# RWKV's low-rank products as two 128-row passes with stored high and low halves, and a gated-delta matrix without its mask

## The chip, the core and the metric

One core of a Trainium2 chip runs the whole program. The metric is device time in microseconds, the median of several executions. TensorE (PE in the profile) does the matrix products, VectorE (DVE) and ScalarE (ACT) the elementwise work, GpSimd (POOL) some small elementwise work, and SyncE (SP) only issues DMA transfers, one after the other in the order of its program. An instruction that waits on an engine holds up everything that stands behind it on that engine; on SP this holds for the transfers behind a waiting transfer.

## What is computed

One layer over 512 positions of width 2048: an input projection, two kinds of sequence mixer side by side (gated delta, 8 heads of 128; RWKV-7, 16 heads of 64, handled here in 8 pairs), an output projection, cross-attention and an MLP. The two places that the change touches:

```python
# RWKV: two low-rank products, rank 64 each
w_log = -softplus(-(w0 + tanh(w_lo) @ w2)) - 0.5
a = sigmoid(a0 + a_lo @ a2)

# gated delta, per chunk: a unit lower triangular system, M strictly lower
gamma = where(causal, exp(where(causal, diff, 0.0)), 0.0)
M = where(strict, einsum("bhnid,bhnjd->bhnij", kb, kc) * gamma, 0.0)
sol = triangular_solve(M + eye, rhs, lower=True, unit_diagonal=True)
```

All data is f32. Big products use an f32r type of matmul and are made of three: each operand is split into a part that f32r holds (high) and the rest (low), and high·high, high·low and low·high are summed.

## The kernel before

The first part of the program, some 1000 us, is one long input projection with the mixers woven into it. The projection is 59 columns of 128 outputs (`py`), each of 16 x 3 matmuls of 128x512 on PE; a column's raw weights come in two halves of 512 KB (`wraw`, three buffers), and ACT and DVE split each half into `whi` and `wlo` (two buffers each) before PE can use it. Seven columns belong to each of eight rounds: three for a pair of RWKV heads, `rwkv(j)`, and four for a gated-delta head, `gdn(h)`. Rounds 1 to 5 are alike.

The order of the instructions in this part isn't written by hand. `run()` is a greedy planner: each stage is a generator of operations, and the planner always takes the one that could start first by its own cost estimates (`cost()`, `start()`, `issue()`), so any change of one operation can move others on all engines, SP's transfers included. On the chip each engine then simply runs its list in that order and waits where an input isn't there yet.

The parts that the prediction follows, in one round:

- `rwkv(j)` loads a 128x128 piece of the stacked weights w2 and a2 (`lw`) and makes `pW` and `pA` by one f32 matmul each over 64 rows: `wa` holds tanh(w_lo) in its upper and a_lo in its lower 64 rows. Later it forms `pgA` and `pgB` on PE, masks them on DVE into `GA` and `GB`, and stores blocks of them to DRAM (`ndri`).
- `inverse_blocks` solves the 16x16 diagonal blocks on POOL. For RWKV: blocks are loaded from DRAM (`sr<-ndri`), POOL works through 15 steps, the results go out to DRAM (`bg16T`, `bg16U`) and come back rearranged (`r<-bg16T` twice, `E<-bg16U` four times). For gated delta the same road has the names `ndgi`, `sgi`, `bg8T`, `bg8U`, `gk<-bg8T`, `gqn<-bg8U`.
- `gdn(h)` turns decays into `E` (exponentials, zero where the row index is above the column index), multiplies it on POOL by the constant `sneg` (minus one strictly above the diagonal, else zero) into `Es`, forms `pkk` on PE and writes the product `NTm = pkk * Es` on DVE (tile name `gEs`). `NTm` goes to DRAM as `ndgi` and through POOL's solve.
- `inverse_levels` joins the solved blocks on PE. Its first products, `gj0x` to `gj7x` by head, need `gk`, the tile that came back from `bg8T`. Since PE runs its list in order, everything behind `gjNx`, the projection too, waits if `gk` isn't there.
- `rs`, `gs`, `po`, `gpo` are the serial recurrences of the mixers, interleaved one by one with projection matmuls.

After this part come the keys and queries of cross-attention (`kp`, `kq`), then the rest, whose order is not touched.

Lines that carry what was just told:

```python
yield TE.matmul(pW, lw[0:64, :], wa[0:64, :], start=True, stop=True)
yield TE.matmul(pA, lw[64:128, :], wa[64:128, :], start=True, stop=True)
```

Of the kernel before, what the change touches and what calls it, by code (L numbers as in the profile page):

```python
# [9 lines left out]
F32 = mybir.dt.float32  # L10
F32R = mybir.dt.float32r
# [6 lines left out]
P = 128  # L18
# [7 lines left out]
CST = {}  # L26
_off = 0
for _n, _w in (("ident", 128), ("ones", 128), ("mA", 128),
               ("lv64", 2 * 64), ("cen", 64), ("sneg", 128), ("mbias", 128),
               ("rst64", 512)):  # L30
    CST[_n] = (_off, _w)
    _off += _w
# [13 lines left out]
def constants():  # L46
    c = np.zeros((P, NCST), np.float32)

    def put(name, a):
        o, w = CST[name]  # L50
        c[:, o:o + w] = a

    i = np.arange(P)
    put("ident", np.eye(P))
    put("ones", 1.0)
    j = np.arange(64)
    st = (j[:, None] < j[None, :]).astype(np.float32)
    inc = (j[:, None] <= j[None, :]).astype(np.float32)
    put("mA", np.tile(np.concatenate([st, inc], 1), (2, 1)))

    def level(n, s):
        a = np.arange(n)
        blk = a[:, None] // (2 * s) == a[None, :] // (2 * s)
        return (blk & (a[:, None] % (2 * s) >= s) & (a[None, :] % (2 * s) < s)).astype(np.float32)

    put("lv64", np.concatenate([np.tile(level(64, 16 << l), (2, 1)) for l in range(2)], 1))
    put("cen", np.tile(np.eye(64) - 1.0 / 64, (2, 1)))
    put("sneg", -(i[:, None] < i[None, :]).astype(np.float32))
    put("mbias", np.where(i[:, None] <= i[None, :], 1e30, -1e30))
    put("rst64", np.tile((np.arange(512) % 64 != 0).astype(np.float32), (P, 1)))  # L70
    return c


def build(tc, I, out):
# [178 lines left out]
    def after(*ev):  # L253
        return lambda: ev in events
# [362 lines left out]
    def rows():  # L617
        R = tl("gE")
        yield DV.memset(R, 0.0)
        rs128 = tl("bon")  # L620
        g8 = slice(32, 40)
        ab, b16 = slice(32, 48), slice(64, 80)
        yield after("rstd")
        yield AC.activation(nA, col("alog"), AF.Exp)
        yield DV.tensor_scalar(out=nA, in0=nA, scalar1=-1.0, scalar2=None, op0=ALU.mult)
        yield DV.memset(rs128[g8, :], 1.0)
        for c in range(4):
            yield DV.memset(rs128[g8, c * P:c * P + 1], 0.0)
# [24 lines left out]
        yield AC.activation(e_[g8, :], e_[g8, :], AF.Ln, bias=b_one[g8, :])
        yield DV.scalar_tensor_tensor(out=x_[g8, :], in0=x_[g8, :], scalar=0.0, in1=e_[g8, :],
                                      op0=ALU.max, op1=ALU.add)
        yield DV.tensor_scalar(out=x_[g8, :], in0=x_[g8, :], scalar1=nA[g8, :], scalar2=None, op0=ALU.mult)
        yield DV.tensor_tensor_scan(out=R[g8, :], data0=rs128[g8, :], data1=x_[g8, :], initial=0.0,
                                    op0=ALU.mult, op1=ALU.add)
        R3 = R.rearrange("p (c t) -> p c t", t=P)
        tail = tl("gqn")  # L660
        t3 = tail.rearrange("p (c t) -> p c t", t=P)
        yield DV.tensor_tensor(out=t3[g8], in0=R3[g8, :, P - 1:P].broadcast_to([8, 4, P]),
                               in1=R3[g8], op=ALU.subtract)
        yield AC.activation(R[96:104, :], tail[g8, :], AF.Exp)
        yield DV.tensor_scalar(out=R[b16, :], in0=R[b16, :], scalar1=0.5, scalar2=0.5, op0=ALU.mult, op1=ALU.add)
        pt = psb("prt", "scg", 1)
        for c in range(4):
            yield TE.transpose(pt[:, c * P:(c + 1) * P], R[:, c * P:(c + 1) * P], ident)
        yield SY.dma_start(Rd, R[32:96, :])
        yield DV.tensor_copy(RT, pt.rearrange("p (c a b) -> p c a b", a=4, b=32)[:, :, 1:4, 0:16])  # L670
# [41 lines left out]
        blk = z.rearrange("(q u) -> q u", u=1040)[:, 0:1024].rearrange("q (r c) -> q r c", c=64)[:, :, 0:16]  # L712
        return full, blk

    def inverse_blocks(nm, store, m, tags, temps, ready, out, moved=False):


        np_ = 4 * m
# [11 lines left out]
        for j in range(15):  # L730
            w = 15 - j
            t = s2[0:np_, 0:w * (j + 1)].rearrange("p (a b) -> p a b", b=j + 1)
            yield GS.tensor_tensor(out=t, in0=D[:, j, j + 1:16].unsqueeze(2).broadcast_to([np_, w, j + 1]),
                                   in1=Td[:, j:j + 1, 0:j + 1].broadcast_to([np_, w, j + 1]), op=ALU.mult)
            yield GS.tensor_tensor(out=Td[:, j + 1:16, 0:j + 1], in0=Td[:, j + 1:16, 0:j + 1], in1=t, op=ALU.add)
        Ud = D
        yield GS.tensor_copy(Ud, Td.rearrange("p a b -> p b a"))
        solving.pop()
# [16 lines left out]
    def inverse_levels(nm, Tm, Tt, NT, tags, mx, big):  # L755
# [4 lines left out]
        for l in range(2):  # L760
# [13 lines left out]
                  for r, c in HI if r == 0 or l == 0]  # L774
            yield from pairs(tl_ + up, th)
            rr = slice(0, P) if l == 0 else hA
            yield DV.tensor_tensor(out=Tm[rr, 0:2], in0=Tm[rr, 0:2], in1=d[rr, 4:6], op=ALU.add)
            yield DV.tensor_tensor(out=Tm[rr, 2:4], in0=Tm[rr, 2:4], in1=o[rr, 0:2], op=ALU.add)
            if l == 0:
                yield DV.tensor_tensor(out=Tt, in0=Tt, in1=d[:, 0:4], op=ALU.add)  # L780
                continue
            for r in (1, 0):
                w = slice(r * 64, r * 64 + 64)
                for c, h in ((slice(0, 2), HALF[r]), (slice(2, 4), HALF[1 - r])):
                    yield DV.tensor_tensor(out=big[HALF[r], c, w], in0=Tt[h, c], in1=d[h, c], op=ALU.add)


    def rwkv(j):
        base = 3 + 7 * j
        js = slice(j * P, (j + 1) * P)  # L790
        lw = tl("lw", P)
        yield SM.dma_start(lw, I["w2a2"][:, js])
        c3 = lambda a: a.rearrange("p (c t) -> p c t", t=64)
        yield after("lowrank")
        yield after("zeros")
        pW, pA = psb(f"pW{j}"), psb(f"pA{j}")
        yield TE.matmul(pW, lw[0:64, :], wa[0:64, :], start=True, stop=True)
        yield TE.matmul(pA, lw[64:128, :], wa[64:128, :], start=True, stop=True)
        tw = short()
        yield AC.activation(tw, pW, AF.Tanh, scale=0.5, bias=hw0[:, j:j + 1])  # L800
        tA = tl("tA")
# [155 lines left out]
        if j < 7:  # L957
            chain(rwkv(j + 1), 3)

        lgs = tile_of(pm, [P, 3 * P], F32R, "lgs", f"lgs{j}", 1)  # L960
        yield AC.copy(lgs[0:96, 0:2 * P], lg[0:96, :])
        yield AC.copy(lgs[96:128, 0:P], lg[96:128, 0:P])
        yield DV.tensor_tensor(out=lgs[:, 2 * P:3 * P], in0=lg[:, 0:P], in1=lgs[:, 0:P].bitcast(F32), op=ALU.subtract)
# [46 lines left out]
    def gdn(h):  # L1010
# [42 lines left out]
            yield DV.scalar_tensor_tensor(out=E[:, cs], in0=E[:, cs], scalar=RT[:, c, 0, h:h + 1],  # L1053
                                          in1=K("mbias"), op0=ALU.subtract, op1=ALU.min)
        yield AC.activation(E, E, AF.Exp)
        Es = tl("gEs")
        yield GS.tensor_tensor(out=c3(Es), in0=c3(E), in1=K("sneg").unsqueeze(1).broadcast_to([P, 4, P]), op=ALU.mult)
        kn = yield from normed(k_, None, "gkn", 0)
        kb = tl("gk")
        yield DV.tensor_tensor(out=kb, in0=kn, in1=B, op=ALU.mult)  # L1060
# [1 line left out]
        for c in range(4):  # L1062
            cs = slice(c * P, (c + 1) * P)
            yield TE.matmul(pkk[:, cs], kn[:, cs], kb[:, cs], start=True, stop=True)
        NTm = Es
        yield DV.tensor_tensor(out=NTm, in0=pkk, in1=Es, op=ALU.mult)

        def store(full):
            yield SY.dma_start(full[:, 0:4, :], c3(NTm)[hA, :, 0:64])
# [1 line left out]

        inv = []
        chain(inverse_blocks(f"gi{h}", store, 8, ("gkn", "gk", "gqn"), lambda: (tl("sgi"), tl("sgj", 240)),
                             after("gq", h), inv, True), 1, ("gi", h))
        if h:
            yield after("gs", h - 1)
        q_ = yield from conv(1, 0, "gq")
# [43 lines left out]
        for c in range(4):  # L1121
            yield TE.matmul(p4[hB, c * 64:(c + 1) * 64], N3[hA, c, 64:128], Tm[hA, c, :], start=True, stop=True)
        Y = tl("gkn")
        yield DV.tensor_copy(Y[hB, 0:256], p4[hB, 0:256])
        p5 = psb(f"gi{h}z", "mg")
        for c in range(4):
            yield TE.matmul(p5[hA, c * 64:(c + 1) * 64], Y[hB, c * 64:(c + 1) * 64], TtG[hB, c, 64:128],
# [918 lines left out]
```

## Time and profile before

| | us |
|---|---|
| median of 3 runs | 2886.73 |
| lowest, highest | 2885.18, 2887.63 |
| the profiled execution | 2890.1 |
| its span in the trace | 2888.3 |
| PE busy in it | 2865.6 |
| DVE, ACT, POOL busy | 2224.1, 1557.9, 312.5 |

The profile comes from one execution, which took 2890.1 us, 3.4 us more than the median; 1.8 us of it lie outside the span. In timelines the columns are start, duration, engine, line, operation, out<-in and count; `SPq` rows are SP issuing transfers. A fp32 matmul shows as two passes, an f32r matmul as one. Starts of neighbouring PE rows show throughput; the durations overlap. Line 228 (`issue`) is the planner's, so almost all of the first part has that line, and rows are told apart by tile names.

### The profile page before, as it was taken

The page shows a single profiled execution, that of the slowest core. Times are in us where ns is not written, and L with a number is a line of the kernel's source. Part 1 is how long each engine was busy: PE and PEld are TensorE (multiplying, and loading weights), DVE is VectorE, ACT ScalarE, POOL GpSimd, SP SyncE. Part 2 cuts the span into 40 slices and gives each one's busy share as a digit, 9 for nine tenths or more (in the row PEclk, how much of TensorE's full clock was granted, in tenths as well). Part 3 has the DMA queues.
Part 4 walks back from the last instruction along what each step waited for, and adds up shares of the span by engine and source line. Part 5 has one row for each costly group of instructions (what it writes and reads, how often), then busy time and mean ns, then how long its engine had stood idle before and what let it go on. Part 6 is the DMA issues. An engine that isn't in the chain of part 4 may idle for free.

```text
span 2888.3 us, 48119 instructions
## 1 busy us (share of the span) xinstructions
PE 2865.6 (99%) x18458; PEld 2412.0 (84%) x18458; DVE 2224.1 (77%) x3379; ACT 1557.9 (54%) x2254; POOL 312.5 (11%) x704
## 2 busy tenths in 40 slices
PE   8999999999999999999999999999999999999998
PEld 7888887888877888889888888888888888888887
DVE  7676676676767767769866898888998896878786
ACT  7454644644646555664455555555555654454444
POOL 0302203213123000001111100010010000000000
PEclk9999999999999999999999999999999999999999
DMA  5423323323424479787788767888777888776765
GB/s 193 112 83 95 99 79 103 93 72 104 114 86 143 155 245 299 261 307 201 206 219 215 187 193 220 229 235 248 215 205 209 290 274 267 222 262 210 252 190 178
DMA packets 304503, 546.64 MB, mean 189 GB/s; under 512 B 97224, under 2 KB 178380, under 8 KB 303248
## 3 DMA queue, kind: packets, MB, share of 16 engines
q1 hardware_dynamic: 245264, 449.17, 49.0%
q0 software_dynamic: 35840, 67.12, 11.7%
q10 hardware_dynamic: 23168, 27.27, 2.6%
q8 instruction: 145, 2.38, 0.3%
q14 instruction: 86, 0.70, 0.1%
HBM read 479.10 MB, written 131.48 MB: 211 GB/s over the span
## 4 chain that ended last, share of the span: by engine, by line
PE 97%; DMA 1%; DVE 1%; POOL 0%; ACT 0%; issue 0%; SPq 0%; ACTq 0%; POOLq 0%
PE py L228 22%; PE upx L1334 8%; PE upx L1336 4%; PE upy L1334 4%; PE dx L1801 4%; PE dx L1800 4%; PE dx L1803 4%; PE vp L122 3%; PE sc L122 3%; PE at L122 3%; PE vo L122 3%; PE kp L228 3%; PE kq L228 3%; PE upy L1336 2%; PE dy L1803 2%; PE dy L1801 2%
## 5 line engine op out<-in xcount | busy, mean ns | idle before, releaser
L130 ACT CAST whi<-ub 128x1024 fp32r<-128x1024 f32 x290 | 304.8, 1052 | 283.8 <-PE dy L1801 62.7
L131 DVE TENSOR_TENSOR wlo<-ub,whi 128x1024 fp32r<-128x1024 f32 x290 | 352.8, 1220 | 63.2 <-ACT whi L130 57.7
L228 PE MATMUL py<-xhi,whi 128*128 128x512 f32 x928 | 374.0, 403 | 7.7 <-ACT xhi L228 7.7
L228 PE MATMUL py<-xlo,whi 128*128 128x512 f32 x928 | 371.2, 400 | 0.0
L228 PE MATMUL py<-xhi,wlo 128*128 128x512 f32 x912 | 363.0, 398 | 0.0
L130 ACT CAST whi<-ua 128x1024 fp32r<-128x1024 f32 x205 | 215.6, 1052 | 195.9 <-PE dx L1801 70.8
L228 ACT CAST whi<-wraw 128x1024 fp32r<-128x1024 f32 (+1 forms) x180 | 187.1, 1039 | 234.6 <-PE py L228 149.4
L131 DVE TENSOR_TENSOR wlo<-ua,whi 128x1024 fp32r<-128x1024 f32 x205 | 249.9, 1221 | 53.4 <-ACT whi L130 52.7
L228 DVE TENSOR_TENSOR wlo<-wraw,whi 128x1024 fp32r<-128x1024 f32 (+1 forms) x178 | 217.6, 1222 | 89.0 <-ACT whi L228 87.6
L1334 PE MATMUL upx<-cb,whi 128*128 128x512 f32 x992 | 250.1, 394 | 0.0
L228 PEld LDWEIGHTS py<-xhi,whi 128*128 128x128 f32 x928 | 174.9, 189 | 48.1 <-ACT xhi L228 7.7
L1334 PEld LDWEIGHTS upx<-cb,whi 128*128 128x128 f32 x992 | 178.5, 189 | 32.5 <-DVE sl L1292 0.4
L228 PEld LDWEIGHTS py<-xlo,whi 128*128 128x128 f32 x928 | 175.1, 189 | 34.5 <-DVE xlo L228 0.7
L228 PEld LDWEIGHTS py<-xhi,wlo 128*128 128x128 f32 x912 | 171.9, 188 | 35.8 <-issue 1.0
L1800 PE MATMUL dx<-whi,dh 128*128 128x512 f32 x480 | 186.8, 389 | 0.0
L1801 PE MATMUL dx<-whi,dl 128*128 128x512 f32 x480 | 186.7, 389 | 0.0
L1336 PEld LDWEIGHTS upx<-cb,wlo 128*128 128x128 f32 x992 | 135.3, 190 | 9.8
L1336 PE MATMUL upx<-cb,wlo 128*128 128x256 f32 x992 | 138.3, 282 | 0.0
L131 DVE TENSOR_TENSOR wlo<-wr,whi 128x1024 fp32r<-128x1024 f32 x80 | 97.8, 1224 | 43.7 <-ACT whi L130 42.7
L1803 PE MATMUL dx<-wlo,dh 128*128 128x512 f32 x480 | 128.6, 389 | 0.0
L228 ACT ACT_TABLE_LOAD x84 | 107.8, 1283 | 35.4 <-DVE suml_gon L228 14.5
L1334 PE MATMUL upy<-cb,whi 128*128 128x512 f32 x496 | 124.3, 392 | 0.0
(903 smaller groups left out, 6681.7 us busy)
## 6 DMA issues: line engine op xcount, KB each, us to landing
ws<-in_w_dn POOLq DMA_DIRECT2D x128, 512.0 KB, 7.4
wraw<-in_w_in SPq DMA_DIRECT2D x116, 512.0 KB, 3.8
ua<-in_w_dn SPq DMA_DIRECT2D x108, 512.0 KB, 4.4
ub<-in_w_up SPq DMA_DIRECT2D x71, 512.0 KB, 6.2
ua<-in_w_up SPq DMA_DIRECT2D x56, 512.0 KB, 4.8
ub<-in_w_dn SPq DMA_DIRECT2D x52, 512.0 KB, 4.6
sl<-cd SPq DMA_DIRECT2D x104, 256.0 KB, 5.0
ub<-ws SPq DMA_DIRECT2D x52, 512.0 KB, 4.3
```

What stands on the lines that cost most here:

```text
L122: PE.matmul(o, l, r, start=start, stop=stop)
L130: tie(S.copy(hi, src))
L131: V.tensor_tensor(out=lo, in0=src, in1=hi.bitcast(F32), op=ALU.subtract)
L228: f(*a, **k)
L1334: PE.matmul(pt, hi[:, k * P:k * P + P], parts[k], start=start and k == 0, stop=False, skip_group_check=True)
L1336: PE.matmul(pt[:, HA], lo[:, k * P:k * P + P], parts[k][:, HA], start=False, stop=k == 7, skip_group_check=True)
L1800: PE.matmul(pts[t], uh[:, x], hi[:, w], start=start and z == 0 and q == 0, stop=False, skip_group_check=True)
L1801: PE.matmul(pts[t], ul[:, x], hi[:, w], start=False, stop=False, skip_group_check=True)
L1803: PE.matmul(pts[t], uh[:, x], lo[:, w], start=False, stop=z == 1 and q == 3, skip_group_check=True)
```

## The change

Two things. First, the low-rank products: `wa` becomes a temporary, and two new f32r tiles hold high and low activations stacked in 128 rows, `LXA` (high part of a_lo in one half of the rows, low part in the other) and `LXW` likewise for tanh(w_lo). The weights are loaded twice, once into each half of the rows, so `lw` is 128x256 and takes four transfers of 64x128 instead of one, and is split into high and low (`lws`: one cast on ACT, one subtraction on DVE). `pW` and `pA` are two f32r matmuls over 128 rows each: weights' high part times the stacked activations, then their low part times the same.

Second, the mask of the gated-delta matrix: `sneg`, its constant columns and POOL's product `Es` go; `NTm = pkk * E` keeps the diagonal and has the other sign. Neither is read wrongly: the solves use only entries strictly above the diagonal of a block, and the signs move into subtractions in place of additions and a multiplication by -1 in place of a copy.

```diff
-    wa = pq.tile([P, T], F32, name="wa")
+    LXW, LXA = (pq.tile([P, T], F32R, name=n) for n in ("LXW", "LXA"))
...
+        wa = tl("gqd")
         yield from shiftmix(0, 0, wa)
         yield AC.activation(wa[0:64, :], wa[0:64, :], AF.Tanh)
+        for x, a, b in ((LXA, hB, hA), (LXW, hA, hB)):
+            yield AC.copy(x[a], wa[a])
+            yield DV.tensor_tensor(out=x[b], in0=wa[a], in1=x[a].bitcast(F32), op=ALU.subtract)
...
-            yield GS.tensor_tensor(out=Td[:, j + 1:16, 0:j + 1], in0=Td[:, j + 1:16, 0:j + 1], in1=t, op=ALU.add)
+            yield GS.tensor_tensor(out=Td[:, j + 1:16, 0:j + 1], in0=Td[:, j + 1:16, 0:j + 1], in1=t, op=op)
...
-        lw = tl("lw", P)
-        yield SM.dma_start(lw, I["w2a2"][:, js])
+        lw = tl("lw", 2 * P)
+        for z, a in enumerate(HALF):
+            for b in HALF:
+                yield SM.dma_start(lw[b, z * P:z * P + P], I["w2a2"][a, js])
+        lws = tile_of(pm, [P, 4 * P], F32R, "lws", f"lws{j}", 1)
+        yield from split_(lw, lws[:, 0:2 * P], lws[:, 2 * P:4 * P])
...
-        yield TE.matmul(pW, lw[0:64, :], wa[0:64, :], start=True, stop=True)
-        yield TE.matmul(pA, lw[64:128, :], wa[64:128, :], start=True, stop=True)
+        for z, (p_, x) in enumerate(((pW, LXW), (pA, LXA))):
+            for n in (0, 1):
+                w = (2 * n + z) * P
+                yield TE.matmul(p_, lws[:, w:w + P], x, start=n == 0, stop=n == 1)
...
-        Es = tl("gEs")
-        yield GS.tensor_tensor(out=c3(Es), in0=c3(E), in1=K("sneg").unsqueeze(1).broadcast_to([P, 4, P]), op=ALU.mult)
...
-        NTm = Es
-        yield DV.tensor_tensor(out=NTm, in0=pkk, in1=Es, op=ALU.mult)
+        NTm = tl("gEs")
+        yield DV.tensor_tensor(out=NTm, in0=pkk, in1=E, op=ALU.mult)
...
-        yield DV.tensor_copy(Y[hB, 0:256], p4[hB, 0:256])
+        yield DV.tensor_scalar(out=Y[hB, 0:256], in0=p4[hB, 0:256], scalar1=-1.0, scalar2=None, op0=ALU.mult)
```

The planner makes a new order of all this. Three places show it. Names have a running number behind them, which differs between the two programs.

On PE, the low-rank products of RWKV's fifth pair, among the first steps of the recurrence of the fourth. Before:

```order
L228 MATMUL py_5323<-xhi_376,wlo_5244 128x512
L228 MATMUL pW_5548<-wa,lw_5546 128x512
L228 MATMUL rs_3_0_5556<-BK_4861,BTz 128x64
L228 MATMUL pA_5549<-wa,lw_5546 128x512
L228 MATMUL py_5323<-xhi_387,whi_5325 128x512
```

Now:

```order
L227 MATMUL gi3y<-gk_5285,gEs_5088 64x64 x3
L227 MATMUL rs_3_1_5628<-Qs_5049,WTz 128x64
L227 MATMUL gi3y<-gk_5285,gEs_5088 64x64
L227 MATMUL pW_5633<-LXW,lws_5606 128x512 x2
L227 MATMUL pA_5634<-LXA,lws_5606 128x512
L227 MATMUL rs_3_1_5638<-BK_4966,BTz 128x64
L227 MATMUL gi3z<-TtG,gkn_5631 64x64 x4
L227 MATMUL pA_5634<-LXA,lws_5606 128x512
```

Two f32 products became four f32r ones, and a step `rs` now stands inside the group `gi3y`, which was whole before.

On SP, the transfers around the end of RWKV's solve and the start of gated delta's in the fourth round. Before:

```order
L228 DMA wraw_4946<-in_w_in 128x1024
L228 DMA bg16T<-sr_4712 64x16x16
L228 DMA bg16U<-sr_4712 64x16x16
L228 DMA r_4953<-bg16T 64x8x64 x2
L228 DMA E_288_4954<-bg16U 64x4x64 x4
L228 DMA wraw_5001<-in_w_in 128x1024
L228 DMA ndgi_5036<-gEs_4892 64x4x64 x2
L228 DMA wraw_5055<-in_w_in 128x1024
L228 DMA sgi_5045<-ndgi_5036 32x16x16
```

Now:

```order
L227 DMA bg16T<-sr_4816 64x16x16
L227 DMA bg16U<-sr_4816 64x16x16
L227 DMA wraw_5047<-in_w_in 128x1024
L227 DMA lg_5063<-in_g2a 128x128
L227 DMA lg_5063<-in_g2b 32x128 x3
L227 DMA r_5051<-bg16T 64x8x64 x2
L227 DMA E_288_5052<-bg16U 64x4x64 x4
L227 DMA wraw_5107<-in_w_in 128x1024
L227 DMA ndgi_5118<-gEs_5088 64x4x64 x2
L227 DMA sgi_5125<-ndgi_5118 32x16x16
```

The five transfers `wraw` and `lg`, which stood ahead of `bg16T`, now stand between `bg16U` and `r`; the `wraw` between `ndgi` and `sgi` is gone. The same rows stand in rounds 2 to 5; in rounds 0 and 1 `lg` stays ahead of `bg16T`.

On DVE, the product that writes `NTm` (tile `gEs`) in the same round. Before:

```order
L228 TENSOR_TENSOR gkn_5003<-gk_4637,sg_4963 128x512
L228 TENSOR_TENSOR gk_5017<-gkn_5003,gqe_4380 128x512
L228 TENSOR_TENSOR gEs_4892<-pkk_5022,gEs_4892 128x512
```

Now:

```order
L227 TENSOR_TENSOR gkn_5055<-gk_4650,sg_4883 128x512
L227 TENSOR_TENSOR gk_5072<-gkn_5055,gqe_4424 128x512
L227 TENSOR_TENSOR y_212<-py_4885,rstd 128x512
L227 TENSOR_TENSOR wlo_5094<-wraw_4828,whi_5093 128x1024
L227 TENSOR_TENSOR gEs_5088<-pkk_5079,gE_4423 128x512
```

An eviction of a projection column and a weight split now stand ahead of it.

Counted on PE in that round: between the last matmul of the second `pgA`/`pgB` group and `pkk` stood 101 f32r matmuls of 128x512, and now 79; between `pkk` and the first `gj3x` stood 123, and now 118. The other groups of matmuls between these points are the same ones. Summed over both stretches, before and now: round 0 227 and 179, round 1 224 and 188, rounds 2 to 5 224 and 197, round 6 220 and 217. In round 1 the groups `ris`, `rit` and `riu` of RWKV now stand ahead of `gj1x` too. The whole program has 12 ACT rows more, of them two table loads.

More of the change, by code (lines that the diff above doesn't have):

```diff
@@ L28 @@
 for _n, _w in (("ident", 128), ("ones", 128), ("mA", 128),
-               ("lv64", 2 * 64), ("cen", 64), ("sneg", 128), ("mbias", 128),
+               ("lv64", 2 * 64), ("cen", 64), ("mbias", 128),
                ("rst64", 512)):
@@ L67, in constants @@
     put("cen", np.tile(np.eye(64) - 1.0 / 64, (2, 1)))
-    put("sneg", -(i[:, None] < i[None, :]).astype(np.float32))
     put("mbias", np.where(i[:, None] <= i[None, :], 1e30, -1e30))
@@ L713, in views, with inverse_blocks @@
         return full, blk
-    def inverse_blocks(nm, store, m, tags, temps, ready, out, moved=False):
+    def inverse_blocks(nm, store, m, tags, temps, ready, out, moved=False, op=ALU.add):
         np_ = 4 * m
@@ L776, in inverse_levels @@
             rr = slice(0, P) if l == 0 else hA
-            yield DV.tensor_tensor(out=Tm[rr, 0:2], in0=Tm[rr, 0:2], in1=d[rr, 4:6], op=ALU.add)
-            yield DV.tensor_tensor(out=Tm[rr, 2:4], in0=Tm[rr, 2:4], in1=o[rr, 0:2], op=ALU.add)
+            yield DV.tensor_tensor(out=Tm[rr, 0:2], in0=Tm[rr, 0:2], in1=d[rr, 4:6], op=ALU.subtract)
+            yield DV.tensor_tensor(out=Tm[rr, 2:4], in0=Tm[rr, 2:4], in1=o[rr, 0:2], op=ALU.subtract)
             if l == 0:
-                yield DV.tensor_tensor(out=Tt, in0=Tt, in1=d[:, 0:4], op=ALU.add)
+                yield DV.tensor_tensor(out=Tt, in0=Tt, in1=d[:, 0:4], op=ALU.subtract)
                 continue
@@ L784, in inverse_levels @@
                 for c, h in ((slice(0, 2), HALF[r]), (slice(2, 4), HALF[1 - r])):
-                    yield DV.tensor_tensor(out=big[HALF[r], c, w], in0=Tt[h, c], in1=d[h, c], op=ALU.add)
+                    yield DV.tensor_tensor(out=big[HALF[r], c, w], in0=Tt[h, c], in1=d[h, c], op=ALU.subtract)
     def rwkv(j):
@@ L958, in rwkv @@
             chain(rwkv(j + 1), 3)
-        lgs = tile_of(pm, [P, 3 * P], F32R, "lgs", f"lgs{j}", 1)
+        lgs = tile_of(pm, [P, 3 * P], F32R, "lgs", f"lg_s{j}", 1)
         yield AC.copy(lgs[0:96, 0:2 * P], lg[0:96, :])
@@ L1073, in gdn @@
         chain(inverse_blocks(f"gi{h}", store, 8, ("gkn", "gk", "gqn"), lambda: (tl("sgi"), tl("sgj", 240)),
-                             after("gq", h), inv, True), 1, ("gi", h))
+                             after("gq", h), inv, True, ALU.subtract), 1, ("gi", h))
         if h:
```

## Prediction

> **What bounds the kernel now.** I read the page first: how busy each engine is, and the chain of work that ended last.
>
> ```profile
> PE 2865.6 (99%) x18458; PEld 2412.0 (84%) x18458; DVE 2224.1 (77%) x3379; ACT 1557.9 (54%) x2254; POOL 312.5 (11%) x704
> PE 97%; DMA 1%; DVE 1%; POOL 0%; ACT 0%; issue 0%; SPq 0%; ACTq 0%; POOLq 0%
> ```
>
> PE is the bound: work taken off PE is time won, work on another engine is free until PE waits for it. So the second view is PE's own waits.
>
> ```profile
> PE py L228 <- ACT xhi L228: 7.7, 1, 7.7
> PE gj6x L228 <- DMA gk<-bg8T: 3.1, 1, 3.1
> ```
>
> Besides the start there is one wait worth a name: in round 6 PE stood 3.1 us before `gj6x`, until gated delta's solved blocks came back from DRAM. The mixers' latency thus already touches PE once. The third view gives busy times by stretch, here a steady round from `pkk` to the next `pkk` (columns: stretch, its length, busy us and count of PE, PEld, DVE, ACT, POOL, then the granted clock).
>
> ```profile
> 453.45:564.53 111.08, 111.08 (x1031) 90.31 (x1030) 75.62 (x141) 57.74 (x79) 24.30 (x67) 1.00 0.32 92
> ```
>
> A round takes 111.1 us, and PE is never idle in it. The question is twofold: how much PE work goes, and whether the new order leaves the chain that ends in `gk` enough time.
>
> **PE work.** PE around the low-rank products of one round:
>
> ```profile
> 497.66 0.39 PE L228 MATMUL py<-xhi,wlo 128*128 128x512 f32 x1
> 497.98 1.12 PE L228 MATMUL pW<-wa,lw 64*128 64x512 f32 x2
> 499.03 0.43 PE L228 MATMUL rs<-BK,BTz 128*128 128x64 f32 x2
> ...
> 500.45 0.50 PE L228 MATMUL py<-xhi,whi 128*128 128x512 f32 x1
> 500.79 0.40 PE L228 MATMUL py<-xlo,whi 128*128 128x512 f32 x1
> 501.02 0.40 PE L228 MATMUL py<-xhi,wlo 128*128 128x512 f32 x1
> 501.26 0.33 PE L228 MATMUL rs<-Qs,WTz 128*128 128x64 f32 x2
> 501.52 0.67 PE L228 MATMUL gi3y<-gk,gEs 64*64 64x64 f32 x8
> ```
>
> An f32r product of 128x512 takes 0.233 us from start to start (500.79 to 501.02). From 497.66 to 500.79 are 3.13 us; without two `py` (0.47) and one `rs` (0.26 by the row at 501.26) the two old products, `pW` and the `pA` that follows `rs`, cost 2.4 us. Four new ones, of the very form of `py`, take 0.93. That saves 1.47. A change to or from a row group of 64 costs about 0.1 (497.66 to 497.98 is 0.32, not 0.23); the `rs` that now splits `gi3y` adds two, and with its lost overlap I take 0.27 back. **1.2 us a round, 9.6 in eight.**
>
> **The chain that ends in `gk`.** One round on SP, DVE and PE, before:
>
> ```profile
> 426.05 0.69 DVE L228 TENSOR_TENSOR GA<-pgA,cst 128x512 f32<-128x512 f32 x1 [0.53 <-PE pgA L228]
> 436.48 0.42 SPq L228 DMA_DIRECT2D lg<-in_g2a  x1
> 436.94 1.43 SPq L228 DMA_DIRECT2D lg<-in_g2b  x3
> 447.00 0.59 SPq L228 DMA_DIRECT2D bg16T<-sr  x1
> 447.68 0.62 SPq L228 DMA_DIRECT2D bg16U<-sr  x1
> 449.76 1.27 SPq L228 DMA_DIRECT2D r<-bg16T  x2
> 451.14 2.55 SPq L228 DMA_DIRECT2D E<-bg16U  x4
> 453.74 0.60 SPq L228 DMA_DIRECT2D wraw<-in_w_in  x1
> 453.46 0.72 PE L228 MATMUL pkk<-gk,gkn 128*128 128x128 f32 x5
> 454.62 0.69 DVE L228 TENSOR_TENSOR gEs<-pkk,gEs 128x512 f32<-128x512 f32 x1 [1.50 <-PE pkk L228]
> 455.34 1.26 SPq L228 DMA_DIRECT2D ndgi<-gEs  x2
> 459.31 0.34 SPq L228 DMA_DIRECT2D sgi<-ndgi  x1
> 476.09 0.34 SPq L228 DMA_DIRECT2D bg8T<-sgi  x1
> 479.14 1.26 SPq L228 DMA_DIRECT2D gk<-bg8T  x2
> 484.77 0.23 PE L228 MATMUL gj3x<-gk,gEs 64*64 64x64 f32 x2
> gk<-bg8T SPq DMA_DIRECT2D x16, 64.0 KB, 2.4
> ```
>
> The reader is to see three things. RWKV's solve leaves POOL 20.95 us after `GA` starts (426.05 to 447.00), and SP then is bound to that solve's four kinds of transfer until 453.74, behind which `ndgi` stands; `NTm` is done only at 455.3, so this costs nothing. From `ndgi` to the landing of the second `gk` transfer (479.14 + 0.64 + 2.4 = 482.2) pass 26.9 us. PE reaches `gj3x` at 484.77: 2.6 us to spare.
>
> Now the order. Between `pgA` and `pkk` stand 22 f32r products fewer, 5.1 us: `pkk` comes 22.3 us after `GA` (before 27.4), that is, `bg16T` 1.3 us ahead of `pkk` instead of 6.5. Behind it SP has, by its rows' steps, `bg16U` 0.7, `wraw` 0.4, `lg` 1.9, `r` 1.4, `E` 2.6, `wraw` 0.4 (the 0.38 of the row at 790.04 below): with 0.7 from `bg16T` to `bg16U`, `ndgi` issues 6.7 us after `pkk`, where it was 1.9. That `NTm` itself stands behind an eviction and a split on DVE changes nothing, since SP comes later still. Then 26.9 us as before: `gk` lands 33.6 us after `pkk`. PE arrives at `gj3x` 31.3 us after `pkk` less five products (1.2), at 30.1. **PE waits 3.4 us a round in rounds 2 to 5**, and `py` waits behind it. Whatever else PE should wait for between `pgA` and `gj3x` is part of this sum, not added to it.
>
> Rounds 0 and 1 lose more products over both stretches, 45 and 36 below the 224 of a steady round where rounds 2 to 5 lose 27, but `lg` (1.9 us) is out of the way there; I take the same 3.4. In all six rounds **20 us**.
>
> Bounds of this wait: had the chain its old slack in full, zero, and then nothing is paid; 1 us more a round if `ndgi` lands late behind the `wraw` issued just ahead of it. Round 6 shows that such a delay exists:
>
> ```profile
> 787.92 0.60 SPq L228 DMA_DIRECT2D wraw<-in_w_in  x1
> 788.62 1.32 SPq L228 DMA_DIRECT2D wraw<-in_memT  x1
> 790.04 0.38 SPq L228 DMA_DIRECT2D wraw<-in_w_in  x1
> 790.50 1.33 SPq L228 DMA_DIRECT2D ndgi<-gEs  x2
> 798.17 0.34 SPq L228 DMA_DIRECT2D sgi<-ndgi  x1
> 820.60:824.10 3.50, 3.50 (x78) 2.63 (x82) 1.06 (x3) 0.69 (x1) 0.00 (x0) 0.57 0.23 46
> ```
>
> Three loads of 512 KB just ahead of `ndgi`, and its landing released `sgi` 7.7 us later instead of 4.0. So came the 3.1 us wait, and behind it 3.5 us at a granted clock of 0.57 (the column behind the busy times), worth 3.5 x 0.43, some 1.5 us. In the new order round 6 keeps 217 of 220 products and gains groups of RWKV ahead of `gj6x`, so I take this event, **4.6 us**, as gone and leave 1 us for what remains of it.
>
> The clock term: waits of 3.4 us are as long as the one that dropped the clock. From none to all six of them could drop it, 0 to 9 us; I take half, **4.5**.
>
> [...]
>
> **The rest.** The `lw` loads and the split:
>
> ```profile
> L228 SPq DMA_DIRECT2D lw<-in_w2a x8: 328/432/432, 11.0 to 826.4; - x8
> L228 ACT CAST lgs<-lg x16: 293/349/408, 163.6 to 933.5; 96x256 fp32r<-96x256 f32 x8, 32x128 fp32r<-32x128 f32 x8
> L228 DVE TENSOR_TENSOR lgs<-lg,lgs x16: 282/292/383, 164.6 to 934.8; 128x128 fp32r<-128x128 f32 x8, 32x128 fp32r<-32x128 f32 x8
> 447.62 1.28 POOL L228 TENSOR_TENSOR gEs<-gE,cst 128x512 f32<-128x512 f32 x1
> L228 ACT ACT_TABLE_LOAD x84 | 107.8, 1283 | 35.4 <-DVE suml_gon L228 14.5
> ```
>
> Three more `lw` issues take 1.3 us of SP a round, a cast near 0.35 us of ACT and a subtraction of 0.3 to 0.7 of DVE (its twice as wide form lies between the quoted row and the 0.69 of `GA`). ACT with 54% and DVE with 77% busy hide them, at zero. The cast waits for `lw`, and weight casts wait behind it, so `py` would pay if `lw` came late; 0 to 1 us a round, I take zero, since `pW` now stands later in its round. The two casts and two subtractions of `LXA` and `LXW` at the start, near 2.6 us at most in series, delay the first `pW` by ten products in PE's order, filled with `py`: zero, or 2.6 without that cover. Two table loads, 2.6 us of ACT: zero. The mask's 1.28 us on POOL stood between the two solves, and the second begins only when `sgi` has landed, 14 us later: no gain. Copy for multiplication, addition for subtraction: the same cost.
>
> **Sum**, against the profiled 2890.1 (span 2888.3, 1.8 outside): -9.6 + 20 - 4.6 + 1 + 4.5 = +11.3, so 2901.4 in a profile. The median of the runs is 3.4 lower: **2898.0**.
>
> **The rivals.**
> - *The waits come, but the clock holds*: +6.8, 2893.5. Against it, the clock row of round 6. [...]
> [...]
> - *The chain is covered, and only PE work counts* (not slower, but faster): the mechanism is SP between `bg16T` and `ndgi`. If `ndgi` issues under 3.3 us after `pkk`, 3.4 earlier than worked out, because the first solve leaves POOL earlier, the waits vanish: -9.6 - 4.6 + 1 = -13.2, 2873.5. For it: PE's old slack of 2.6 us. Against it: five transfers more stand there by the order, and POOL runs the same 15 steps.
> - That the new products don't run as four of 0.233 is excluded by the `py` rows of that form.
>
> **How the numbers follow.** Chances: forecast 0.48, clock holds 0.12, half the wait 0.22, covered 0.18. About 0.2%, 5.8 us, is what a measurement can tell from no change; so slower 0.60, same 0.22, faster 0.18. The forecast's own range is 2892 (no clock term, and waits of 3 us) to 2909 (all six drop the clock, +4.5, and 1 us more a round, +6). The 8-in-10 range reaches down through the half wait and most of the way to the covered case: 2877 to 2910.
>
> **What would show it.** `PE gj0x` to `gj5x` waiting on `gk<-bg8T` for 2.5 to 4 us each in PE's waits; `ndgi` 6 to 7 us after `pkk`; a granted clock below 1 behind some of them; four low-rank products at 0.233. A round of 113 us confirms the waits, one of 109.9 refutes them. The forecast is wrong if PE shows no wait at `gjNx`, or waits elsewhere, at `pW` for `lws`.

## The result, and the profile after

| | before | after |
|---|---|---|
| median, us | 2886.35 (4 runs, 2885.18 to 2887.63) | 2920.59 (4 runs, 2918.65 to 2924.96) |
| ratio, 95% interval | | 1.0118 (1.0106 to 1.0131) |
| the profiled execution, us | 2890.1 | 2920.12 |
| its span, us | 2888.3 | 2918.3 |

The kernel became 34.2 us slower; the forecast was 11.3 us slower than the profile of before, 2901.4 in a profile and 2898.0 in the median. The page's first and fourth parts, after:

```profile
PE 2867.9 (98%) x18458; PEld 2422.1 (83%) x18458; DVE 2224.0 (76%) x3389; ACT 1563.0 (54%) x2266; POOL 318.5 (11%) x696
PE 88%; DMA 4%; POOL 3%; DVE 2%; issue 1%; SPq 1%; ACT 1%; POOLq 0%; ACTq 0%; DVEq 0%
```

Before, 97% of the chain that ended last was PE, now 88%: the shares of DMA, POOL and DVE have grown. PE's busy time is 2.3 us longer although PE has less to do, a first sign of a lower clock (granted clock 0.994 in the mean, before 0.999). PE's own waits (in total, times, longest us):

```profile
PE gj2x L227 <- DMA gk<-bg8T: 5.4, 2, 5.1
PE gj5x L227 <- DMA gk<-bg8T: 4.8, 1, 4.8
PE gj4x L227 <- DMA gk<-bg8T: 4.8, 2, 4.5
PE gj0x L227 <- DMA gk<-bg8T: 4.5, 1, 4.5
PE gj3x L227 <- DMA gk<-bg8T: 4.5, 2, 4.3
PE ri7x L227 <- DMA r<-bg16T: 2.3, 2, 2.0
PE gn L227 <- DVE suml_gn L227: 1.8, 1, 1.8
PE gj6t L227 <- DMA gqn<-bg8U: 1.6, 1, 1.6
PE py L227 <- DVE wlo L227: 1.5, 1, 1.5
```

Five rounds wait at `gjNx` for `gk<-bg8T`, 24.0 us in all, where the forecast had six rounds and 20; round 1, in which `ndgi` came 2.6 us after `pkk`, has none. Four smaller waits were not forecast. The fourth round on SP, with three rows of PE and DVE (start, duration):

```profile
471.96 0.58 SPq L227 DMA_DIRECT2D bg16T<-sr  x1
472.63 0.62 SPq L227 DMA_DIRECT2D bg16U<-sr  x1
473.31 0.65 SPq L227 DMA_DIRECT2D wraw<-in_w_in  x1
474.01 0.43 SPq L227 DMA_DIRECT2D lg<-in_g2a  x1
474.48 1.36 SPq L227 DMA_DIRECT2D lg<-in_g2b  x3
475.95 1.27 SPq L227 DMA_DIRECT2D r<-bg16T  x2
477.32 3.25 SPq L227 DMA_DIRECT2D E<-bg16U  x4
480.67 0.55 SPq L227 DMA_DIRECT2D wraw<-in_w_in  x1
481.32 1.25 SPq L227 DMA_DIRECT2D ndgi<-gEs  x2
485.29 0.33 SPq L227 DMA_DIRECT2D sgi<-ndgi  x1
...
504.50 1.26 SPq L227 DMA_DIRECT2D gk<-bg8T  x2
472.09 1.05 PE L227 MATMUL pkk<-gk,gkn 128*128 128x128 f32 x8
475.15 0.68 DVE L227 TENSOR_TENSOR gEs<-pkk,gE 128x512 f32<-128x512 f32 x1
506.94 0.44 PE L227 MATMUL gj3x<-gk,gEs 64*64 64x64 f32 x2 [4.28 <-DMA gk<-bg8T]
```

`NTm` (the row `gEs<-pkk`) is ready at 475.83, and `ndgi`, which stores it, issues at 481.32. Nothing holds it but SP: every row of SP from 473.31 to 480.67 is somebody else's transfer. `ndgi` comes 9.2 us after `pkk` (1.9 before), and PE waits from 502.7 to 506.94.

The waits cost more than their length. By the windows (stretch, its length, busy us of PE, PEld, DVE, ACT, POOL, then the granted clock), the stretch at that place and the whole round:

```profile
504.47:511.29 6.82, 4.16 (x81) 3.84 (x82) 1.38 (x4) 0.00 (x0) 0.00 (x0) 0.50 0.33 77
472.09:588.38 116.29, 111.82 (x1031) 92.16 (x1030) 75.41 (x142) 57.88 (x80) 26.10 (x67) 0.97 0.32 88
```

The clock is halved for 6.8 us, in 4.2 of which PE is busy. By the clock record this happened for 6.83 us behind the waits of rounds 0, 2 and 3 and for 3.41 us behind those of 4, 5 and `ri7x`: 30.7 us, in which PE stood idle for 6.9, so (30.7 - 6.9) / 2 = 11.9 us lost, against 1.5 in the kernel before. (An estimate: it takes PE's work in such a period to need half the time at full clock. A `py` product stepped 0.43 us there, 160.28 to 160.71, against 0.23.) A round takes 116.3 us, not the 113 that the forecast named.

### The profile page after: what moved, and what is told of

It reads as the page before. It is cut to its first block, busy times and chain, and to the rows that moved or that the text cites. A ratio compares the mean times of both kernels' runs of the same rounds, so it can differ in the third digit from the quotient of the medians.

```text
span 2918.3 us, 48181 instructions
## 1 busy us (share of the span) xinstructions
PE 2867.9 (98%) x18458; PEld 2422.1 (83%) x18458; DVE 2224.0 (76%) x3389; ACT 1563.0 (54%) x2266; POOL 318.5 (11%) x696
## 4 chain that ended last, share of the span: by engine, by line
PE 88%; DMA 4%; POOL 3%; DVE 2%; issue 1%; SPq 1%; ACT 1%; POOLq 0%; ACTq 0%; DVEq 0%
PE py L227 16%; PE upx L1341 8%; PE upx L1343 4%; PE upy L1341 4%; PE dx L1808 4%; PE dx L1807 4%; PE dx L1810 4%; PE kq L227 3%; PE vp L121 3%; PE sc L121 3%; PE at L121 3%; PE vo L121 3%; PE kp L227 3%; PE upy L1343 2%; PE upz L1341 2%; PE dy L1807 2%
```

## The experiments

The theories, as they stood at the start. **A**: the planner's new order gives the chain from `GA` to `gk` too little time, whatever the cause in that order. **B**: the chain itself became slower on the chip by the changed operations. **C**: the low-rank part's loads and split make the loss. Theory A later split into two: too few projection products between `pgA` and `gjNx` (**count**), or the place of gated delta's transfers on SP (**SP**). A third outcome, **shift**, is that the wait only moves to `riNx`, which needs RWKV's `r`. In the table, `gj` is the sum of PE's waits at `gjNx` for `gk`, all waits are PE's waits up to the end of `kq`, the one at the start included, and half clock is the time at a granted clock of 0.5 in that part. These three columns, in us, come from the one execution of each kernel that was profiled. The ratio is to runs of the kernel before that were taken beside it, with medians of 2886.3 to 2887.0.

| run | median us | ratio to before (95%) | gj | all waits | half clock |
|---|---|---|---|---|---|
| before | 2886.35 | | 3.1 | 13.0 | 3.4 |
| after | 2920.59 | 1.0118 (1.0106 to 1.0131) | 24.3 | 39.8 | 30.7 |
| e1 mask alone | 2904.16 | 1.0059 (1.0044 to 1.0074) | 5.4 | 19.6 | 10.2 |
| e2 low-rank alone | 2914.47 | 1.0097 (1.0082 to 1.0112) | 5.8 | 35.4 | 23.9 |
| e3 after, POOL 350 | 2881.08 | 0.9979 (0.9969 to 0.9988) | 1.2 | 13.2 | 0 |
| e4 before, POOL 350 | 2897.68 | 1.0038 (1.0025 to 1.0051) | 0 | 16.1 | 20.5 |
| e5 `ndgi` behind `bg16U` | 2928.22 | 1.0144 (1.0129 to 1.0159) | 32.8 | 47.9 | 44.4 |
| e6 `ndgi` ahead of `bg16T` | 2930.02 | 1.0152 (1.0137 to 1.0168) | 34.6 | 47.6 | 47.8 |
| e7 only `lg`, `wraw` behind | 2920.96 | 1.0121 (1.0105 to 1.0136) | 27.6 | 42.5 | 37.5 |
| e8 after, POOL 450 | 2897.35 | 1.0035 (1.0023 to 1.0048) | 0 | 19.0 | 17.1 |
| e9 `sgi` too | 2885.34 | 0.9994 (0.9985 to 1.0003) | 0.9 | 17.6 | 0 |
| e10 `sgi` too, `ndgi` first | 2884.69 | 0.9992 (0.9982 to 1.0002) | 0.4 | 16.5 | 3.4 |
| e11 before, `sgi` too | 2893.08 | 1.0023 (1.0012 to 1.0034) | 2.2 | 17.0 | 0 |
| e12 both repairs | 2879.98 | 0.9979 (0.9969 to 0.9988) | 0 | 13.5 | 0 |

### Each part alone

e1 takes the low-rank part of the change back, e2 the mask's; against the kernel after, first e1 and then e2:

```diff
-        lw = tl("lw", 2 * P)
+        lw = tl("lw", P)
+        yield SM.dma_start(lw, I["w2a2"][:, js])
...
+        yield TE.matmul(pW, lw[0:64, :], wa[0:64, :], start=True, stop=True)
+        yield TE.matmul(pA, lw[64:128, :], wa[64:128, :], start=True, stop=True)
```

```diff
+        Es = tl("gEs")
+        yield GS.tensor_tensor(out=c3(Es), in0=c3(E), in1=K("sneg").unsqueeze(1).broadcast_to([P, 4, P]), op=ALU.mult)
...
+        yield DV.tensor_tensor(out=NTm, in0=pkk, in1=Es, op=ALU.mult)
```

Expected of e1:

> The kernel after with the low-rank part put back as it was before (one transfer for lw, two f32 products), so only gated delta's mask is gone. Theory A (the planner's order leaves the chain from GA to gk too few projection products between pgA and gjNx): the order has 198 and 184 such products in rounds 0 and 1, 206 in round 2 and 227 in rounds 3 to 5, so waits at gj0x and gj1x of 3 to 4 us, at most 1 to 2 in round 2, none in rounds 3 to 5; with the clock behind two waits about +3 to +6 us on the kernel before, 2886 to 2893. Theory B (the chain itself has become slower on the chip, by the changed operations on DVE and POOL, whatever the order): waits in all rounds as in the kernel after, some of its 34 us in this part, 2895 or more. Theory C (the low-rank part alone makes the loss by its loads and its split): no waits at all here, 2886 or a little less.

Expected of e2:

> The kernel after with gated delta's mask put back (sneg, the product Es on POOL, additions as before), so only the low-rank products are new. Theory A: between pgA and gjNx stand 179, 233, 187, 168, 169, 215, 175 products in rounds 0 to 6, so waits in rounds 0, 2, 3, 4 and 6, the longest in 3, 4 and 6 (6 to 10 us where 50 products are missing), none in round 1, at most 1 in round 5; in all some 24 us of waits and with the clock a time of 2905 to 2925. Theory B: waits do not follow the count of products; they would be alike in all rounds, 1 and 5 too. Theory C: the loss of the kernel after is all here, 34 us, in waits at pW or py for lws or wlo and not at gjNx.

Each part alone makes the kernel slower, by 17.8 and 28.1 us, which don't add up to the 34.2 of both: each makes a new order of the whole projection part. Two of the waits of e1, then three of e2:

```profile
PE gj0x L227 <- DMA gk<-bg8T: 3.8, 2, 3.4
PE gj1x L227 <- DMA gk<-bg8T: 1.6, 2, 1.3
...
PE py L228 <- DVE y L228: 9.2, 2, 5.0
PE gj0x L228 <- DMA gk<-bg8T: 3.1, 1, 3.1
PE gj3x L228 <- DMA gk<-bg8T: 1.0, 1, 1.0
```

e1 waits where the count said (rounds 0 and 1, none in 3 to 5), so theories B and C fall: the mask alone, which takes an operation away, makes waits, and only in the two rounds with the fewest products. Its time was 11 us above the upper end expected, a miss; in its profile stand small waits at other places and 10.2 us at half clock. e2 speaks against a plain count of projection products: in round 3 it has 168 of them between `pgA` and `gj3x`, 29 fewer than the kernel after, and waits 1.0 us there in place of 4.5. But `gk` came no earlier in it (`gj3x` starts 35.9 us after `pkk`, in the kernel after 34.9). PE came later: groups of RWKV's `ri` products stand ahead of `gj3x` in this order, and PE is through with its work only 34.8 us after `pkk`, against 30.6. The count leaves such groups out. e2's time lies within what theory A gave, but for another reason: the 9.2 us at `py` for `y` are in round 6 (from 820 to 846 us), a place that no theory had, and 20.5 of its 23.9 us at half clock come behind 820 us.

### The order repaired through the planner's number

```diff
-            return 116 + 0.75 * n if nm == "memset" else 235 + 2.3 * n
+            return 116 + 0.75 * n if nm == "memset" else 350 + 2.3 * n
```

This in the kernel after is e3, in the kernel before e4, and with 450 in the kernel after e8.

> The kernel after, with one number of the planner changed: an elementwise operation on POOL is planned at 350 ns and 2.3 ns an element in place of 235 ns, so that the planner allows the POOL solves about the time that they take on the chip and puts more projection products between pgA and gjNx (189 to 229 a round). Every instruction of the kernel after is there, only their order differs. Theory A: no waits at gjNx over 1 us, no low clock behind them, and the 9.6 us of PE work saved comes through: 2876 to 2884. Theory B (the chain on the chip is late by the changed operations themselves): waits of 2 us or more in most rounds, 2900 or more.

> The control of the last one: the kernel before with the same number of the planner changed (242 to 255 products between pgA and gjNx). Theory A: the chain was covered before, so only the wait of round 6 and the clock behind it can go: 2881 to 2887. If the new number is good or bad for the order by itself, apart from the chain, it shows here as a difference from the kernel before, and what the change is worth in this order is this run against the last.

> The kernel after with the planner's number for an operation on POOL at 450 ns and 2.3 ns an element (209 to 243 products between pgA and gjNx). Theory SP: what counts is that ndgi stands ahead of r and E on SP and comes 2 to 4 us after pkk; if it does here too, no waits at gjNx over 1 us and 2876 to 2886. Against it: the more products stand between, the more of the small ones come together elsewhere, and waits or the low clock turn up at other places: 2890 or more, as in the kernel before with 350.

With every instruction of the change in it, e3 is 39.5 us faster than the kernel after and beats the kernel before by 5.3, within what theory A gave. Theory B is excluded by it. It speaks against the count once more: in round 3 e3 has 197 products between `pgA` and `gj3x`, exactly as many as the kernel after, and no wait there. PE reaches `gj3x` 2.3 us later than in the kernel after, with `ri` products ahead of it, which covers half of the 4.3 us; the second `gk` transfer issues 6.4 us earlier (26.7 us after `pkk`, against 33.1). What differs ahead of it is SP. Some rows of the fourth round of e3 on SP:

```profile
456.37 1.24 SPq L227 DMA_DIRECT2D ndgi<-gEs  x2
457.89 0.57 SPq L227 DMA_DIRECT2D bg16T<-sr  x1
459.09 0.57 SPq L227 DMA_DIRECT2D bg16U<-sr  x1
460.06 0.33 SPq L227 DMA_DIRECT2D sgi<-ndgi  x1
...
462.20 3.28 SPq L227 DMA_DIRECT2D E<-bg16U  x4
...
480.32 1.51 SPq L227 DMA_DIRECT2D gk<-bg8T  x2
```

`ndgi` and `sgi` are through before `E` begins. e4, the control, missed its expectation by 11 us on the slow side: it has no wait at `gjNx` at all, yet 20.5 us at half clock (see the last section) in its profiled execution, which took 6.2 us more than the median. With this number of the planner the two kernels are thus 2897.7 - 2881.1 = 16.6 us apart, more than the PE work, but they don't share one order, and some 10 us of it are the half clock in that execution of e4. e8 came out as the second of its two expectations: no waits at `gjNx`, but 17.1 us at half clock in one stretch of round 6. In rounds 2 to 5 of e8 `sgi` issues 14 us after `pkk`, as late as in the kernel after (13.1 to 14.7), and yet PE doesn't wait, since it comes to `gjNx` only 47 us after `pkk`: more work ahead of `gjNx` covers the chain as well as a faster chain does. The number that plans POOL better is no safe repair by itself; one order came out well, two did not.

### SP's order alone

The next runs leave PE, DVE, ACT and POOL in exactly the order of the kernel after and move only transfers on SP, in rounds 0 to 5. In the planner's `issue()` a transfer that is to follow is kept back and issued behind the one it follows. This is e9, shortened:

```diff
-        f(*a, **k)
+        sp, go = eng == "SP" and hold["n"] < 6, lambda: f(*a, **k)
...
+        elif sp and o_.startswith("sgi"):
+            go()
+            hold["n"] += 1
+            for x in hold["q"]:
+                x[1]()
...
+        elif sp and hold["on"]:
+            hold["q"].append((o_, go))
+        else:
...
+            go()
+            if sp and o_.startswith("bg16U") and i_.startswith("sr"):
+                hold["on"] = True
```

In e5 to e7 the kept transfers go out behind the second `ndgi` already; in e7 only `lg` and `wraw` are kept; in e6 and e10 keeping begins with `bg16T` itself.

> The kernel after with one thing changed in rounds 0 to 5: on SP, ndgi is issued right behind bg16U, and the transfers wraw, lg, r and E that stood between the two follow it. PE, DVE, ACT and POOL run exactly the order of the kernel after. Theory SP (the wait at gjNx comes from ndgi standing behind RWKV's transfers on SP, not from too few products between pgA and gjNx): ndgi issues some 4 us after pkk in rounds 2 to 5 in place of 9 to 10 (bounded then by NTm on DVE, 3.1 us after pkk), the four waits of 4.3 to 5.1 us go, and with them the low clock behind them; round 0 keeps most of its 4.5, since there bg16T itself comes late. 2920.6 - 18.7 - some 9 of the clock: 2890 to 2897. Theory count (197 products are too few whatever SP does): waits over 2 us stay in rounds 2 to 5, 2908 or more. Theory shift (the wait moves to PE's ri products, since r lands 3 to 4 us later): waits at riNx, 2905 or more.

> As the last one, but ndgi is issued ahead of bg16T too, so that nothing of RWKV's solve stands before it; the other engines run the order of the kernel after. Theory SP: round 0 too loses its wait (NTm is done 1.1 us after pkk there, bg16T only 3.3 after), rounds 2 to 5 are as in the last one; what is left against the run with the planner's other number are the waits at ri7x, gn and gj6t: 2883 to 2890. Theory count: no gain on the last one, waits stay. Theory shift: bg16T now waits for ndgi, r lands up to 5 us later, and PE waits at riNx for r: slower than the last one.

> As the first of these, but only lg and wraw (the five transfers that the change moved, and one more wraw) are put behind ndgi; r and E stay ahead of it. Theory SP with the moved transfers as the cause: the waits of rounds 2 to 5 go by the 3 us that these transfers take, to 1.5 us or less, and the clock holds: 2893 to 2900. Theory SP with RWKV's own r and E as the larger part (r can't issue before bg16T has landed, 2.8 us behind it, and r and E take 4.6 us): ndgi comes only 2 us earlier, 7.3 us after pkk, waits of some 2.5 us stay, and half of the clock's loss: 2900 to 2910.

All three missed: e5 and e6 are slower than the kernel after, e7 like it. Rows of round 3 of e5 on SP, and POOL's first step of the solve in the kernel after and in e5, show why (the line numbers are those of the three places in `issue()` from which a transfer now goes out):

```profile
483.27 0.62 SPq L244 DMA_DIRECT2D bg16U<-sr  x1
486.52 1.24 SPq L231 DMA_DIRECT2D ndgi<-gEs  x2
...
491.76 2.56 SPq L238 DMA_DIRECT2D E<-bg16U  x4
494.41 0.55 SPq L238 DMA_DIRECT2D wraw<-in_w_in  x1
495.00 0.43 SPq L244 DMA_DIRECT2D sgi<-ndgi  x1
...
515.96 1.24 SPq L244 DMA_DIRECT2D gk<-bg8T  x2
487.28 0.20 POOL L227 TENSOR_TENSOR sgj<-sgi 32x15 f32<-32x15 f32 x1 [14.25 <-DMA sgi<-ndgi]
499.19 0.66 POOL L244 TENSOR_TENSOR sgj<-sgi 32x15 f32<-32x15 f32 x1 [15.52 <-DMA sgi<-ndgi]
```

`ndgi` did come 5.4 us earlier against `pkk` (3.8 for 9.2), but the transfers that had stood ahead of it now stood between it and `sgi`, which still issued 12.3 us after `pkk` (13.2 in the kernel after). This 0.9 us was lost again behind it: POOL, which waits for `sgi` to land, began 4.2 us after its issue (495.00 to 499.19), against 2.0 in the kernel after (485.29 to 487.28). In rounds 2 to 5 of e5 to e7 it is 4.1 to 5.7 us, and a `wraw` of 512 KB stands 0.5 or 0.6 us ahead of `sgi`; in the kernel after it is 2.0 to 2.3, and the last `wraw` ahead is 4.6 to 5.3 us away. That this `wraw` holds up `sgi` fits the rows, but wasn't tested by itself. The theory had looked at one transfer of the road and not at the next.

> The kernel after with SP's order changed further in rounds 0 to 5: bg16T, bg16U, ndgi twice and then sgi at once; wraw, lg, r and E follow sgi. The other engines run the order of the kernel after. The three runs with ndgi alone moved left wraw, lg, r and E between ndgi and sgi, so sgi came 12.3 us after pkk there (13.2 before that move, 5 to 6 in the kernel before). Theory SP, mended (the whole road bg16U, ndgi, sgi has to be free of RWKV's transfers): sgi 7.5 us after pkk in rounds 2 to 5, POOL done some 4 to 6 us earlier, gk landed about when PE arrives (30.2 us after pkk): waits of 0 to 1.5 us there, 2 in round 0, little low clock: 2887 to 2897. Theory count (too few products between pgA and gjNx whatever SP does): waits over 3 us stay, 2910 or more. Theory shift: r lands some 7 us later and PE waits at riNx, 2905 or more.

> As the last one, but in the order ndgi twice, bg16T, bg16U, sgi, and then the rest. Theory SP, mended: round 0 gains too (ndgi 1.8 us after pkk in place of 4.4, sgi near 5.3), so all waits at gjNx are at most 1.5 us: 2883 to 2892. Theory count: waits over 3 us, 2910 or more. Theory shift: waits at riNx for r.

Rows of round 3 of e9 on SP, and the round behind it by the windows:

```profile
458.91 0.62 SPq L230 DMA_DIRECT2D bg16U<-sr  x1
462.14 1.75 SPq L230 DMA_DIRECT2D ndgi<-gEs  x2
465.48 0.33 SPq L230 DMA_DIRECT2D sgi<-ndgi  x1
...
469.64 2.56 SPq L230 DMA_DIRECT2D E<-bg16U  x4
...
483.18 1.24 SPq L230 DMA_DIRECT2D gk<-bg8T  x2
568.60:678.50 109.90, 109.90 (x1032) 90.26 (x1031) 75.58 (x142) 57.90 (x80) 23.69 (x67) 1.00 0.35 93
```

`sgi` 7.1 us after `pkk`, no wait at `gj0x` to `gj5x`, no time at half clock, 35.3 us faster than the kernel after, and all of it from the place of some twelve transfers a round on one queue. The time is 1.7 us below what was expected of e9, and e10 is not told apart from it. The theory count (too few products, whatever SP does) falls, since the products are those of the kernel after, and so does the shift of the wait to `riNx`: `r` was issued 6 us later than in the kernel after, and PE never waited for it in these rounds.

> The control of the run with sgi right behind ndgi: the kernel before with the same rule on SP in rounds 0 to 5 (bg16T, bg16U, ndgi twice, sgi, then wraw, r and E); its other engines keep their order. Theory SP: in the kernel before gk lands 2.6 us ahead of PE and no round of these waits, so the rule can win nothing: 2884 to 2890, and what the change is worth with SP out of the way is the difference to the run of the kernel after with this rule. If the rule is a gain by itself (ndgi to gk is shorter when sgi follows at once), it shows only as more slack at gjNx, 2 to 4 us. If it harms (r, E and one wraw come 8 us later), waits at py for wlo or at riNx: over 2890.

> Both repairs together: the kernel after in the order with the planner's other number for POOL, and sgi right behind ndgi on SP. Theory SP: that order had a wait of only 0.9 us left at gj4x and 0.3 at gj2x, so at most 1.2 us can go: 2878 to 2883. If wraw comes too late behind sgi, waits at py for wlo: 2884 or more.

The rule is no gain by itself: the kernel before with it is 2893.1, 3 us above what was expected of it and slower by some 6 us (waits of 3.0 us at `gn` and 2.1 at `pqk`, where it had 0.3 and none). With the chain out of the way on both sides the two kernels are 2893.1 - 2885.3 = 7.8 us apart; that isn't the change's PE work alone, since those waits are in it. e12, both repairs together, is not told apart from e3; 2880 us is the best of these kernels, 6.9 us below the kernel before that ran beside it.

## Why the prediction failed, step by step

The sum, term by term, in the profiled executions (change against before, us):

| term | forecast | measured |
|---|---|---|
| PE work | -9.6 | -8.8 (what remains in the projection part) |
| waits at `gj0x` to `gj5x` | +20 | +24.0 |
| wait of round 6 | -2.1 | -2.8 |
| all other waits of PE there | 0 | +5.6 |
| clock | +3.0 | +10.4 |
| behind the projection part | 0 | +1.6 |
| sum | +11.3 | +30.0 |

(The forecast's round-6 event of -4.6 is split here into its wait of 3.1 and its clock of 1.5; the clock's +4.5 - 1.5 = +3.0. The last products of `kq` ended 28.4 us later than before, so -8.8 is 28.4 less the waits and the clock; +1.6 is the rest of the 30.0 by which the span grew.) Of the 18.7 us that the sum is short, the clock is 7.4, waits at other places 5.6 and the waits at `gjNx` 4.0.

- **PE work: right.** The undisturbed rounds of e9 and e10 take 109.9 to 110.2 and 109.7 us, against 111.08 before: 0.9 to 1.4 a round for the 1.2 of the forecast. After, the products run as the four of the `py` form that were expected.

```profile
523.87 0.73 PE L227 MATMUL pW<-LXW,lws 128*128 128x512 f32 x2
524.44 0.40 PE L227 MATMUL pA<-LXA,lws 128*128 128x512 f32 x1
```

- **The chain: right in its place and mechanism, the size somewhat low.** SP between `bg16T` and `ndgi` was named, and PE reaches `gj3x` about when it was worked out: its last `py` ahead of it ends at 502.7, 30.6 us after `pkk`, for 30.1. But "`ndgi` issues 6.7 us after `pkk`" was 9.2: `bg16T` issued 0.1 us ahead of `pkk` rather than 1.3, `E` took 3.25 us for 2.55, and the steps of the two `wraw` came to some 1.35 for 0.8. The road from `ndgi` to the landing was 25.6 us for 26.9, which gave some 1.2 of this back. So rounds 2 to 5 wait 4.3 to 5.1 us, and round 0 4.5, for the 3.4 forecast; round 1 was wrong the other way. The half wait of the chances (1.7 us a round, no clock term) came in no round.
- **The covered rival's condition was incomplete.** It said that the waits vanish if `ndgi` issues early enough, and took the 26.9 us behind it as fixed. In round 1 of e5 and in rounds 0 and 1 of e6 `ndgi` issued 1.8 us after `pkk`, within the 3.3 that were asked, and PE waited 3.5 to 4.1 us all the same, because `sgi` has a place on the same queue. With `sgi` right behind `ndgi` (e9, fourth round) the second `gk` transfer issues 21.7 us after the first `ndgi`, against 24.5 in the kernel before and 30.1 in e5.
- **The clock: the step that failed most.** That waits of this length would drop the clock was right; the size, "I take half, 4.5", measured 11.9. Not half of the waits but all five of 4.3 to 5.1 us halved the clock, in three rounds for 6.83 us and in two for 3.41, which cost 10.2 us; another 1.7 came behind the wait at `ri7x`. The forecast had also read the price of a drop, 1.5 us, off a single wait with 3.41 us behind it. The rival that the clock holds was wrong.
- **"Startup zero" and round 7 left out.** The waits of `py` for `wlo` (1.5, at 54 us) and for `wGB` and `wGA` (0.8, near 23 us) come from the start, which had been bounded at 2.6 and taken at zero; `ri7x` (2.3), `gn` (1.8 for 0.3) and `gj6t` (1.6) are places of rounds 6 and 7 that the forecast didn't look at, although the counted order was new there too. What each of them comes from was not tested one by one; e9 and e10 keep `ri7x`, `gn`, `gj6t` and the start's `wlo` at 1.0 to 1.9 us each, so SP's order in rounds 0 to 5 doesn't make them.
- **The subtraction of 3.4 us for the median** held for the kernel before alone: the profiled run of the kernel after lies 0.5 us below its median. This is 3.9 of the 22.6 us between 2898.0 and 2920.6.
- **Mask, `lw` loads, table loads at zero**: nothing in PE's waits contradicts it; no wait names `lws`, `pW` or `pA`. The changed operations cost much the same: on DVE the copy into `gkn` from `gi0y` to `gi6y` took 427 ns and the multiplication takes 428 or 429, the 64x128 addition into `gk` from `gj0u` to `gj6u` took 278 to 280 ns and the subtraction takes the same. On POOL the solve's additions (`sgi<-sgi,sgj`) took 288 ns in the median and its subtractions 295, while the multiplications beside them (`sgj<-sgi`), which the change leaves alone, went from 271 to 280.

## What to carry to other kernels

A transfer queue that runs in order belongs to the critical path as soon as a chain passes through it: add up everything that stands on it between the chain's first and last transfer, and look at all of the chain's transfers together. Here moving `ndgi` alone was worth nothing (e5), and moving `sgi` with it was worth 35 us (e9). A small saving on the bound engine, here 1.2 us a round, is won only if the order that a planner makes anew keeps the latency chains covered; counting projection products between two points told this only in part (e1), and the places of `ndgi` and `sgi` on SP, with the time at which PE arrives, told the rest. A wait of PE should be priced with the clock: here 24 us of waits came with 27 us at half clock, some 10 us lost.

## What the runs showed of the hardware that was not expected

Half clock without idle time. Ahead of two of the drops in e4 the profile shows PE busy throughout the 3.4 us before. Ends of matmuls are modelled, so short gaps would not show. The windows of these two (PE busy first, granted clock behind POOL), and rows of what PE ran ahead of the first:

```profile
170.60:174.00 3.40, 3.40 (x23) 2.18 (x23) 1.43 (x5) 0.69 (x1) 0.00 (x0) 1.00 0.07 22
174.00:180.83 6.83, 6.83 (x17) 4.65 (x16) 3.90 (x7) 3.34 (x5) 0.00 (x0) 0.50 0.00 0
286.65:290.06 3.41, 3.41 (x18) 1.68 (x17) 2.10 (x7) 0.69 (x1) 0.00 (x0) 1.00 0.00 0
290.06:293.47 3.41, 3.41 (x11) 2.91 (x11) 1.23 (x3) 1.23 (x2) 0.00 (x0) 0.50 0.00 0
...
171.56 1.12 PE L228 MATMUL pW<-wa,lw 64*128 64x512 f32 x2
...
172.98 0.67 PE L228 MATMUL gi0z<-TtG,gkn 64*64 64x64 f32 x8
173.59 1.69 PE L228 MATMUL pA<-wa,lw 64*128 64x512 f32 x2
```

In the 3.4 us ahead of the first stand the two old low-rank products, which use 64 rows, and small products; no product of 128x512 over 128 rows starts in them. In all e4 has 20.5 us at half clock, near 10 us lost, in a kernel whose waits in that part are only 3 us longer than those of e3. e8 was at half clock for 17.1 us in round 6, behind 13.7 us in which PE was busy for 8.7; in the last 10.3 of these it ran nearly only small products, most of them 64x64. Idle time of PE stands ahead of other drops: in the 3.41 us ahead of each drop of the kernel after PE was busy for 0.00 (round 5) to 1.67 us (`ri7x`), and ahead of the one drop of the kernel before for 0.66. What sets the clock is not shown by these runs.

How long the clock stayed low in the kernel after did not follow the length of a wait. Behind the waits of rounds 0, 2 and 3 (4.5, 5.1 and 4.3 us) it was at 0.50 for 6.83 us, and PE was idle for another 1.9 to 2.7 us in the first half of that. Behind those of rounds 4 and 5 (4.5 and 4.8 us) it was at 0.50 for 3.41 us, and PE was idle for 0.1 us in it.
